# When the modulation rows of a two-layer hybrid are computed: from the first key block on, with a pause before layer 1

## The chip, the cores and the metric

One core of a Trainium2 chip runs the whole program. The metric is the device time of one execution in microseconds; of the kernel before there are three, from 2134.82 to 2137.38 with a median of 2135.68.

## The reference: what is computed

A model of two layers on 256 latent rows and 256 context rows of width 2048, in float32. A vector c modulates both layers: `silu(c)` is multiplied by wide matrices, which gives a shift, a scale and a gate of 2048 numbers for each layer.

```python
h = norm(x) * (1 + scale) + shift          # shift, scale, gate = silu(c) @ ada[layer]
layer 0: q,k,v,z,ab,b,c,h,z2 = h @ w_in    # 16 heads of gated DeltaNet, both directions, and a short convolution
layer 1: chunk MLP (two gelu halves, layer norm over 2048, a 128-row mixing matrix) and a pool of four radii
x = x + gate * (y @ w_out)
```

Layer 1's shift and scale are wanted when layer 1 begins, its gate only in the last output projection.

## The kernel before

Each float32 weight block of 512 KB (a chunk: 128 partitions x 1024) is loaded by a DMA that SyncE issues, split by ScalarE into a high part H (L202) and by VectorE into a low part L = raw - H (L209), and TensorE multiplies three times: H by the high activations, L by the high ones, H by the low ones (L234 in `proj`, L243 to L245 in `projT_n`). `wchunk` does the load and the split for all 554 chunks. In the order of VectorE's list, chunks 0 to 31 are the first projection, 32 to 71 the key and value blocks (`wkv`), 72 to 263 the four head groups of layer 0 (head groups 0 to 3), 264 to 327 its output projection, and the rest is layer 1.

The modulation rows are 256 units in the background of that stream. `ada_step` issues a 256 KB load of 128 rows x 512 columns (L273, SyncE) and, four units behind, one VectorE instruction that multiplies it by silu(c) and adds it to an accumulator (L281; every sixteenth starts one, L279); after 16 units TensorE sums over the partitions (`adc`, L287), ScalarE copies (L289) and a small matmul (L291) and VectorE put the row away. `wchunk` calls it: `tick[0]` is a rate per chunk, taken from `RATE` by stage (`tick[2]`): 0 key blocks, 1 head groups, 2 output projection of layer 0, 3 layer 1. In stage 2 it stops at 198 steps (12*16+2+4), which finish all but layer 1's gate. Before layer 1, L1015 makes up what is missing to 198, since L1016 reads the scale.

The instructions are written in this order, and a scheduler then reorders each engine's list by its own model of times; an engine executes its list in order.

At the layer boundary `out_proj` multiplies the last block by the gate (`opt`, L668), adds it to x (L669) and lets ScalarE square and sum (L670). `row_rstd` (L992, L993, and ten small instructions of `rsqrt`, L337 to L341, 128x1 each) gives the reciprocal root of a row, `dg` (L1022) is a diagonal matrix of it, and TensorE turns x by it (`tr`, L1027); from the turned tile come h, and the first matmuls of layer 1. This is done for the two halves n = 0 and n = 1. At the end of each head group the state scan ends in a chain `z` (L894), `az` (L916), a norm, and the transposes `oT` (L933). In layer 1, `wsT`, `lnw` and `lnb` are loads that GpSimd issues for the layer norm and the mixing (`sp`, L1160).

Of the kernel before, what the change touches and what calls it, by code (L numbers as in the profile page):

```python
# [14 lines left out]
ALU = mybir.AluOpType  # L15
# [4 lines left out]
KT = 16  # L20
# [9 lines left out]
HP = 1  # L30
LA = 4
FINK = 2
RATE = (2.5, 0.6, 1.2, 0.4)
LP = (0.0, 0.0, 0.0, 0.0)
CHUNKS = (1, 2, 4, 4, 5)
RADII = (1, 2, 4, 8)
# [86 lines left out]
def body(ctx: ExitStack, tc: tile.TileContext, T, dbg=None):  # L123
    nc = tc.nc
    dbg = dbg or {}
    V, S, PE, G = nc.vector, nc.scalar, nc.tensor, nc.gpsimd
# [3 lines left out]
    def pool(name, bufs=1, space=None, stack=ctx, side=None):  # L130
        kw = {} if space is None else {"space": space}
        if space is None:
            kw["reuse_waits"] = "tile"
        if side is not None:
            kw["side"] = side
        return stack.enter_context(tc.tile_pool(name=name, bufs=bufs, **kw))
# [56 lines left out]
    tick = [0.0, 0.0, 0, 0.0]  # L193

    def wchunk(src, nk, rp=None, hp=None, lp=None, sz=1024, HL=None):
        if extra[0] and hp is None:
            extra[1] += 1
            rp, hp, lp = extra[0][extra[1] % len(extra[0])]
        raw = (rp or wrawp).tile([P, sz], F32, name="raw", tag="raw")
        dma(raw, src)  # L200
        H = HL[0] if HL else (hp or whp).tile([P, sz], F32R, name="H", tag="H")
        S.copy(H, raw)  # L202
        L = HL[1] if HL else (lp or wlp).tile([P, sz], F32R, name="L", tag="L")
        tick[3] += LP[tick[2]]
        if tick[3] >= 1.0:
            tick[3] -= 1.0
            G.tensor_tensor(L, raw, H, ALU.subtract)
        else:
            V.tensor_tensor(L, raw, H, ALU.subtract)  # L209
        tick[1] += tick[0]  # L210
        while tick[1] >= 1.0:
            tick[1] -= 1.0
            if tick[2] != 2 or ada_n[0] < 12 * KT + FINK + LA:
                ada_step()
        return [t.rearrange("p (k c) -> p k c", k=nk) for t in (H, L)]

# [6 lines left out]
    def proj(src, cols, acts, outs, shared, kts=KT):  # L223
        nk = 1024 // cols
        for c in range(kts // nk):
            H, L = wchunk(src[:, c * 1024:(c + 1) * 1024], nk)
            for kk in range(nk):
                k = c * nk + kk
                for n, o in enumerate(outs):
                    st = k == 0 and n % shared == 0  # L230
                    sp = k == kts - 1
                    wH, wL = (t[:, kk, n * P:(n + 1) * P] for t in (H, L))
                    for i, (w, t) in enumerate(((wH, 0), (wH, 1), (wL, 0))):
                        PE.matmul(o, w, acts(t, k),  # L234
                                  start=st and i == 0, stop=sp and i == 2, skip_group_check=True)
# [31 lines left out]
    araw, aacc, ada_n = {}, {}, [0]  # L267

    def ada_load(u):
        w, col = segs[u // 64][:2]  # L270
        k, col = u % KT, col + u // KT % 4 * 512
        araw[u] = adap.tile([P, 512], F32, name="araw", tag="araw", bufs=LA)
        dma(araw[u], w[k * P:(k + 1) * P, col:col + 512])  # L273

    def ada_acc(u):
        k, raw = u % KT, araw.pop(u)
        if k == 0:
            aacc[u // KT] = adap.tile([P, 512], F32, name="acc", tag="acc", bufs=2)
            V.tensor_scalar(aacc[u // KT], raw, cs[:, 0, 0:1], None, ALU.mult)  # L279
        else:  # L280
            V.scalar_tensor_tensor(aacc[u // KT], raw, cs[:, k, 0:1], aacc[u // KT], ALU.mult, ALU.add)  # L281

    def ada_fin(s):
        out0, gate = segs[s // 4][2:]
        t = gp.tile([P, 132], F32, name="adc", tag="g")
        for n in range(4):
            PE.matmul(t[32 * n:32 * n + 32, 0:P], ones[:, 0:32], aacc[s][:, n * P:(n + 1) * P], start=True, stop=True)  # L287
        ts = adap.tile([P, P], F32, name="ads", tag="ads")
        S.copy(ts, t[:, 0:P])  # L289
        t = t[:, P:132]  # L290
        PE.matmul(t, ts, sel4, start=True, stop=True)  # L291
        c4 = out0 + 4 * (s % 4)
        V.tensor_tensor(modc[:, c4:c4 + 4], t, adabc[:, c4:c4 + 4], ALU.add)
        if gate is not None and s % 4 == 3:
            t = gp.tile([P, P], F32, name="adr", tag="g")
            PE.transpose(t[0:KT], modc[:, out0:out0 + KT], ident)
            r = adap.tile([KT, P], F32, name="arow", tag="ads")
            S.copy(r, t[0:KT])
            dma(rowd[gate].rearrange("(a b) -> a b", a=KT), r)
# [3 lines left out]
    def ada_step(n=1):  # L303
        for _ in range(max(0, min(n, ADA_N - ada_n[0]))):
            u = ada_n[0]
            if u < 256:
                ada_load(u)
            if LA <= u < 256 + LA:
                ada_acc(u - LA)
            f = u - KT - FINK - LA + 1  # L310
            if f >= 0 and f % KT == 0:
                ada_fin(f // KT)
            ada_n[0] += 1
# [54 lines left out]
    with ExitStack() as ph1:  # L368
# [3 lines left out]
        with ExitStack() as ph0:  # L372
# [69 lines left out]
            def k_load(e, j):  # L442
                return [t[:, 0] for t in wchunk(T["wset"][e, j], 1, rp=k0r, hp=whp, lp=wlp, sz=768)]
# [146 lines left out]
        def finish(b, ps):  # L590
            grp, kv, half = b // 4, b // 2 % 2, b % 2
            for n in range(2):
                h = grp * 4 + half * 2 + n
                w = conv5[:, 16 + 16 * kv + h, :]
                ft = cp.tile([P, 512], F32, name="kvT", tag="kvT")
                conv_silu(cp, ft, ps[:, n, :], w, 512)
                tr = gp.tile([P, 4, P], F32, name="kvp", tag="g")
                for m in range(4):
                    PE.transpose(tr[:, m, :], ft[:, m * P:(m + 1) * P], ident)
                tk = cp.tile([P, 4, P], F32, name="kvt", tag="kvt")  # L600
                if kv == 0:
                    dma(ktd[h], ft)
                    S.copy(tk, tr)
                    jk = cp.tile([P, P], F32, name="jk", tag="jk")
                    for m in range(4):
                        S.activation(jk, tk[:, m, :], AF.Square, accum_out=ksq[:, m, h:h + 1])
                    dma(kkd[h], tk.rearrange("p a b -> p (a b)"))
                else:
                    V.tensor_tensor(tk, tr, nrs[:, :, h:h + 1].to_broadcast([P, 4, P]), ALU.mult)
                    dma(vvd[h], tk.rearrange("p a b -> p (a b)"))  # L610
            if b % 4 == 1:
                hs = slice(grp * 4, grp * 4 + 4)
                V.tensor_scalar(kr2[:, :, hs], ksq[:, :, hs], EPS, None, ALU.add)
                rsqrt(nrs[:, :, hs], kr2[:, :, hs])
                V.scalar_tensor_tensor(nrs[:, :, hs], nrs[:, :, hs], -1.0, kr2[:, :, hs], ALU.mult, ALU.mult)
                V.reciprocal(kr2[:, :, hs], kr2[:, :, hs])

        early = [0, 1, 4, 5, 8, 9]
        for step, b in enumerate((12, 13, 2, 3, 6, 7, 10, 11, 14, 15)):
            if step == 3:  # L620
                tick[0], tick[2] = RATE[0], 0
            ps = pj.tile([P, 2, 512], F32, name="pj", tag="pj")
            proj(T["wkv"][b // 4, b // 2 % 2, b % 2], 256, both, [ps[:, n, :].rearrange("p (s t) -> p s t", s=2) for n in range(2)], 1)
            if early:
                finish(early.pop(0), acc[step])
            finish(b, ps)
            if step == 6:
                ab_rows()
                hx = hxp.tile([P, 2, KT, 256], F32R, name="hx", tag="hx")
            if step > 6:  # L630
                for t in range(2):
                    for q in range(1 if step < 9 else 2):
                        k4 = slice(4 * (step - 7 + q), 4 * (step - 6 + q))
                        S.copy(hx[:, t, k4], hxc[:, 0, t, k4])
# [45 lines left out]
    hxH, hxL = hx[:, 0], hx[:, 1]  # L680
    tick[0], tick[2] = RATE[1], 1
    KTp = pool("ktp", 2, stack=y_stack, side="right")
# [304 lines left out]

    tick[0], tick[2] = RATE[2], 2

# [59 lines left out]

    tick[0], tick[2] = RATE[3], 3  # L1050
    Wk = pool("wk1", 2)
# [175 lines left out]
```

## Time and profile before

| | |
|---|---|
| profiled execution: time, span | 2136.03 us, 2134.3 us |
| median of three | 2135.68 us |
| TensorE matmuls busy | 2051.9 us, 96% |
| TensorE weight loads busy | 84% |
| VectorE busy | 1546.9 us, 72% |
| ScalarE busy | 1024.3 us, 48% |
| all loads and stores | 446 MB, mean 209 GB/s |

The time lies 1.7 us above the span. TensorE is idle for 82.4 us of the span. A modulation unit costs VectorE one instruction (`acc`), TensorE next to nothing, and the DMA queue one load. In a timeline a row's time is from its start to its recorded end, and the next may start a little earlier; in the waits the releaser is the instruction whose end let the engine go on.

### The profile page before, as it was taken

To read this page: it belongs to the slowest core of one execution; us is meant where nothing else is said; L and a number is where in the kernel's file an instruction comes from. 1 tells how busy PE (TensorE), PEld (TensorE's weight loads), DVE (VectorE), ACT (ScalarE), POOL (GpSimd) and SP (SyncE) were. 2 spreads that over 40 slices of the span, in tenths; PEclk is the share of its full clock that TensorE was granted. 3 is DMA by queue.
4 is the path that set the end of the run, shared out by engine and by line. 5 is a ranking of instruction groups with operands and counts; after the bars stand their busy time and mean duration, and the time that the engine had idled before them with its cause. 6 is when DMAs were issued, how large, how long until landed. Compare 5 with 4: busy or idle time off the path is not lost. (4 is left out here: it accounts for less than half of the span.)

```text
span 2134.3 us, 37062 instructions
## 1 busy us (share of the span) xinstructions
PE 2051.9 (96%) x14414; PEld 1785.0 (84%) x14414; DVE 1546.9 (72%) x2767; ACT 1024.3 (48%) x1764; POOL 34.0 (2%) x51
## 2 busy tenths in 40 slices
PE   6999999999999999989999999898999999999998
PEld 4667888889999999889999778677888888888886
DVE  4435997877976899579759984798687886665554
ACT  5223366325554556445646554445454555444443
POOL 0000000000000000000000000000010000000000
PEclk9999999999999999999999999999999999999999
DMA  9776745777644785366457752897765666667663
GB/s 347 265 257 211 233 158 187 248 245 268 184 131 147 256 269 159 120 211 186 132 157 245 268 178 70 286 319 270 264 213 168 189 189 198 197 192 222 193 194 131
DMA packets 151248, 446.09 MB, mean 209 GB/s; under 512 B 16512, under 2 KB 23456, under 8 KB 150048
## 3 DMA queue, kind: packets, MB, share of 16 engines
q1 hardware_dynamic: 145936, 425.37, 61.5%
q0 software_dynamic: 5136, 18.35, 2.7%
q8 instruction: 113, 1.85, 0.4%
q14 instruction: 63, 0.52, 0.1%
HBM read 423.19 MB, written 20.46 MB: 208 GB/s over the span
## 5 line engine op out<-in xcount | busy, mean ns | idle before, releaser
L202 ACT CAST H<-raw 128x1024 fp32r<-128x1024 f32 (+1 forms) x554 | 575.3, 1042 | 719.3 <-PE pj L234 215.7
L209 DVE TENSOR_TENSOR L<-raw,H 128x1024 fp32r<-128x1024 f32 (+1 forms) x554 | 667.4, 1207 | 340.6 <-ACT H L202 331.7
L234 PE MATMUL pj<-hx,H 128*128 128x256 f32 x3072 | 562.6, 283 | 0.0
L234 PEld LDWEIGHTS pj<-hx,H 128*128 128x128 f32 x3072 | 476.1, 189 | 3.2 <-issue 0.6
L234 PE MATMUL pj<-hx,L 128*128 128x256 f32 x1536 | 434.9, 283 | 0.0
L1076 PE MATMUL pj<-h,H 128*128 128x512 f32 x1024 | 361.1, 396 | 2.2 <-DVE jn L1085 2.2
L234 PEld LDWEIGHTS pj<-hx,L 128*128 128x128 f32 x1536 | 290.3, 189 | 2.1 <-issue 1.0
L1078 PE MATMUL pj<-h,L 128*128 128x256 f32 x1024 | 287.9, 281 | 0.0
L1076 PEld LDWEIGHTS pj<-h,H 128*128 128x128 f32 x1024 | 192.7, 188 | 46.9 <-DVE jn L1085 2.5
L234 PE MATMUL pj<-hxc,H 128*128 128x512 f32 x640 | 204.9, 399 | 0.0
L281 DVE SCALAR_TENSOR_TENSOR acc<-araw,cs,acc 128x512 f32<-128x512 f32 x240 | 178.8, 745 | 25.3 <-DMA araw<-in_ada 13.7
L1078 PEld LDWEIGHTS pj<-h,L 128*128 128x128 f32 x1024 | 194.2, 190 | 0.2 <-issue 0.2
L234 PEld LDWEIGHTS pj<-hxc,H 128*128 128x128 f32 x640 | 119.5, 188 | 28.2 <-issue 0.8
L234 PE MATMUL pj<-hxc,L 128*128 128x512 f32 x320 | 127.5, 398 | 0.0
L450 PE MATMUL pj<-hxc,H 128*128 128x512 f32 (+1 forms) x272 | 87.6, 397 | 0.0
L243 PE MATMUL pj<-H,y 128*128 128x512 f32 x192 | 76.0, 396 | 0.0
L244 PE MATMUL pj<-L,y 128*128 128x512 f32 x192 | 75.9, 396 | 0.0
L245 PE MATMUL pj<-H,y 128*128 128x512 f32 x192 | 75.9, 396 | 0.0
L234 PEld LDWEIGHTS pj<-hxc,L 128*128 128x128 f32 x320 | 60.3, 188 | 14.0
L450 PEld LDWEIGHTS pj<-hxc,H 128*128 128x128 f32 x272 | 49.8, 193 | 14.4 <-issue 4.5
L387 PE MATMUL adm<-raw,cs 128*32 128x256 f32 x512 | 42.3, 407 | 16.9 <-DMA raw<-in_ada 16.9
L243 PE MATMUL pj<-H,yb 128*128 128x512 f32 x128 | 51.4, 401 | 3.7 <-ACT H L202 2.6
(399 smaller groups left out, 3093.6 us busy)
## 6 DMA issues: line engine op xcount, KB each, us to landing
raw<-in_wbb SPq DMA_DIRECT2D x128, 512.0 KB, 3.8
raw<-in_wout SPq DMA_DIRECT2D x128, 512.0 KB, 3.8
araw<-in_ada SPq DMA_DIRECT2D x192, 256.0 KB, 4.6
raw<-in_ada SPq DMA_DIRECT2D x64, 512.0 KB, 6.5
raw<-in_wpz SPq DMA_DIRECT2D x64, 512.0 KB, 3.7
raw<-in_wuz SPq DMA_DIRECT2D x64, 512.0 KB, 4.2
raw<-in_wkv SPq DMA_DIRECT2D x40, 512.0 KB, 4.4
araw<-in_ada0g SPq DMA_DIRECT2D x64, 256.0 KB, 4.0
```

What stands on the lines that cost most here:

```text
L202: S.copy(H, raw)
L209: V.tensor_tensor(L, raw, H, ALU.subtract)
L234: PE.matmul(o, w, acts(t, k), start=st and i == 0, stop=sp and i == 2, skip_group_check=True)
L243: PE.matmul(o, xH[:, t], H[:, kk, :], start=st, stop=False, skip_group_check=True)
L244: PE.matmul(o, xH[:, t], L[:, kk, :], start=False, stop=False, skip_group_check=True)
L245: PE.matmul(o, xL[:, t], H[:, kk, :], start=False, stop=sp, skip_group_check=True)
L281: V.scalar_tensor_tensor(aacc[u // KT], raw, cs[:, k, 0:1], aacc[u // KT], ALU.mult, ALU.add)
L387: PE.matmul(m[32 * kk:32 * kk + 32, 0:256], cs32[:, 4 * c + kk, :], raw[:, kk * 256:(kk + 1) * 256], start=c == 0, stop=c == 3, skip_group ...
L450: PE.matmul(ps[n].rearrange("p (s t) -> p s t", s=2)[:, q], w_, hxc[:, q, t, j, :], start=first and i == 0 and srcs[0] == 0, stop=last and ...
L1076: PE.matmul(ps[:, n], H[:, kk, w], x[:, :, k, :], start=k == 0, stop=k == kts - 1, skip_group_check=True)
L1078: PE.matmul(ps[:, n, 0], L[:, kk, w], x[:, 0, k, :], start=False, stop=k == kts - 1, skip_group_check=True)
```

## The change

The key blocks start the background steps at the first block (step 0 of the ten) and no longer at the fourth. The limit of 198 steps holds in stages 0, 1 and 2. In stage 3 each step is issued behind the low part of its chunk by `tc.issue_after`, at a rate of one step in two chunks in place of two in five.

```diff
-RATE = (2.5, 0.6, 1.2, 0.4)
+RATE = (2.5, 0.6, 1.2, 0.5)
...
-            V.tensor_tensor(L, raw, H, ALU.subtract)
+            low = V.tensor_tensor(L, raw, H, ALU.subtract)
         tick[1] += tick[0]
         while tick[1] >= 1.0:
             tick[1] -= 1.0
-            if tick[2] != 2 or ada_n[0] < 12 * KT + FINK + LA:
+            if tick[2] == 3:
+                with tc.issue_after(low.ins):
+                    ada_step()
+            elif ada_n[0] < 12 * KT + FINK + LA:
                 ada_step()
...
-            if step == 3:
+            if step == 0:
                 tick[0], tick[2] = RATE[0], 0
```

The scheduler's lists change throughout. Units accumulated when the VectorE list has come to a chunk's low part, before and now: chunk 47: 32 and 32; chunk 60: 45 and 73; chunk 70: 68 and 96; chunk 90: 96 and 127; chunk 262: 165 and 194; chunk 331: 214 and 194; chunk 353: 256 and 205; chunk 455: 256 and 256. Lines of the changed kernel stand three higher behind L216.

VectorE at the layer boundary, before, from the sum of the squares for n = 0 on (`rst` and `rsy` are the small tiles of the reciprocal root, `acc` is a modulation unit, `x_1` the second half):

```order
L992 TENSOR_REDUCE rst_4196<-sq_4195 128x1
L281 SCALAR_TENSOR_TENSOR acc<-araw,cs,acc 128x512
L668 TENSOR_TENSOR opt<-pg,gts 128x512
L209 TENSOR_TENSOR L<-raw,H 128x1024
L993 TENSOR_SCALAR rsq_4197<-rst_4196 128x1
L209 TENSOR_TENSOR L<-raw,H 128x1024
L281 SCALAR_TENSOR_TENSOR acc<-araw,cs,acc 128x512
L669 TENSOR_TENSOR x_1_15075<-x_1_15075,opt 128x512
L337 TENSOR_SCALAR rsy<-rsq_4197 128x1
L281 SCALAR_TENSOR_TENSOR acc<-araw,cs,acc 128x512
L339 TENSOR_TENSOR rst<-rsy 128x1
L992 TENSOR_REDUCE rst_4196<-sq_4195 128x1
```

and now, from the instruction behind that sum to the `dg` of n = 0:

```order
L996 TENSOR_SCALAR rsq_4297<-rst_4296 128x1
L340 TENSOR_SCALAR rsy<-rsq_4297 128x1
L342 TENSOR_TENSOR rst<-rsy 128x1
L343 SCALAR_TENSOR_TENSOR rst<-rst,rsq_4297 128x1
L344 SCALAR_TENSOR_TENSOR rsy<-rst,rsy 128x1
L342 TENSOR_TENSOR rst<-rsy 128x1
L343 SCALAR_TENSOR_TENSOR rst<-rst,rsq_4297 128x1
L344 SCALAR_TENSOR_TENSOR rsy<-rst,rsy 128x1
L342 TENSOR_TENSOR rst<-rsy 128x1
L343 SCALAR_TENSOR_TENSOR rst<-rst,rsq_4297 128x1
L344 SCALAR_TENSOR_TENSOR rst_4296<-rst,rsy 128x1
L1025 TENSOR_SCALAR dg<-cst,rst_4296 128x128
```

Three modulation units, two low parts and the other half's `opt` and `x`, which stand in the first piece, are not between the steps of this chain any more; three low parts and that `opt` and `x` stand behind the `dg`.

TensorE at the end of head group 2, before (`pj` is a projection, `oT` the transposes, `adc` a sum of the modulation rows):

```order
L234 MATMUL pj<-hx,L 128x256
L234 MATMUL pj<-hx,H 128x256 x2
L234 MATMUL pj<-hx,L 128x256
L933 MATMUL oT<-cst,on 128x128 x4
L234 MATMUL pj<-hx,H 128x256
L933 MATMUL oT<-cst,on 128x128 x4
L287 MATMUL adc<-acc,cst 32x128 x8
L234 MATMUL pj<-hx,H 128x256
L234 MATMUL pj<-hx,L 128x256
L234 MATMUL pj<-hx,H 128x256 x2
```

and now (`rq` and `G` are the first matmuls of the next group):

```order
L237 MATMUL pj<-hx,L 128x256
L897 MATMUL z<-r,U 128x128 x4
L919 MATMUL az<-zs,aT 128x128 x4
L936 MATMUL oT<-cst,on 128x128 x8
L290 MATMUL adc<-acc,cst 32x128 x8
L722 MATMUL rq<-qs,cst 32x256 x4
L752 MATMUL G<-KTt 128x128 x4
L294 MATMUL adc<-cst,ads 128x4
L727 MATMUL rq<-cst,rs 128x4 x2
L237 MATMUL pj<-hx,H 128x256 x2
```

The last projection matmul before the next group stands ahead of `z`, `az` and `oT` now, where before projections stood on both sides of `oT`.

## Rows read from the trace of the kernel before

**Rows 1.** The page, part 1: busy time, share, instructions of each engine.

```profile
PE 2051.9 (96%) x14414; PEld 1785.0 (84%) x14414; DVE 1546.9 (72%) x2767; ACT 1024.3 (48%) x1764; POOL 34.0 (2%) x51
```

**Rows 2.** TensorE's waits, whole span: line, releaser; total, times, longest, us.

```profile
PE oT L933 <- DVE on L930: 13.1, 2, 6.6
...
PE Sp L905 <- ACT zk L898: 4.3, 6, 1.6
...
PE az L916 <- ACT zs L901: 2.9, 4, 0.7
...
PE sp L1160 <- DMA wsT<-in_wsT: 2.3, 1, 2.3
```

**Rows 3.** Windows at the layer boundary: busy us (instructions), clock, DMA.

```profile
1437.20:1445.70 8.50, 0.00 (x0) 0.03 (x1) 8.47 (x31) 1.77 (x3) 0.00 (x0) 0.62 0.86 267
1445.70:1449.40 3.70, 3.70 (x17) 3.70 (x18) 1.98 (x5) 0.46 (x1) 0.00 (x0) 0.50 0.80 292
```

**Rows 4.** Groups of VectorE, 360.3 to 372.57: count, busy us, mean ns, idle before.

```profile
L281 DVE SCALAR_TENSOR_TENSOR acc<-araw,cs,acc 128x512 f32<-128x512 f32 x8 | 6.0, 752 | 3.5 <-DMA araw<-in_ada0g 3.3
```

**Rows 5.** Timeline of TensorE across the boundary: start, us, work, idle before.

```profile
1436.76 0.39 PE L245 MATMUL pg<-H,yaL 128*128 128x512 f32 x1
1445.70 5.61 PE L1027 MATMUL tr<-dg,x 128*128 128x128 f32 x32 [8.55 <-issue]
...
1452.49 0.48 PE L243 MATMUL pj<-H,h 128*128 128x512 f32 x1
...
1465.88 0.40 PE L243 MATMUL pj<-H,h 128*128 128x512 f32 x1
```

**Rows 6.** Timeline of ScalarE there, the squares of the last x.

```profile
1435.36 0.62 ACT L670 ACTIVATE opt<-x 128x512 f32<-128x512 f32 x1
```

**Rows 7.** Timeline of VectorE there.

```profile
1434.80 0.74 DVE L281 SCALAR_TENSOR_TENSOR acc<-araw,cs,acc 128x512 f32<-128x512 f32 x1
1435.49 1.22 DVE L209 TENSOR_TENSOR L<-raw,H 128x1024 fp32r<-128x1024 f32 x1
1436.63 0.15 DVE L992 TENSOR_REDUCE rst<-sq 128x1 f32<-128x4 f32 x1
...
1445.31 0.28 DVE L1022 TENSOR_SCALAR dg<-cst,rst 128x128 f32<-128x128 f32 x1
```

**Rows 8.** Timeline of VectorE, a reciprocal root that nothing interrupts.

```profile
1339.13 0.17 DVE L344 TENSOR_SCALAR oss<-oss 128x8 f32<-128x8 f32 x1 [2.59 <-ACT on L925]
...
1341.34 0.17 DVE L928 TENSOR_TENSOR fac<-fac,rqs 128x8 f32<-128x8 f32 x1
```

**Rows 9.** Windows: layer norm, end of head group 1, and twice head group 3.

```profile
1594.00:1611.00 17.00, 11.74 (x51) 9.70 (x50) 10.92 (x22) 4.58 (x6) 3.35 (x7) 0.80 0.57 183
925.00:930.60 5.60, 5.60 (x35) 4.43 (x35) 4.75 (x9) 0.92 (x3) 0.00 (x0) 0.50 0.40 110
1150.00:1170.00 20.00, 20.00 (x164) 19.65 (x163) 20.00 (x50) 12.82 (x40) 0.00 (x0) 1.00 0.78 245
1190.00:1205.00 15.00, 10.93 (x49) 8.29 (x49) 13.85 (x23) 8.53 (x10) 0.00 (x0) 0.89 0.86 290
```

**Rows 10.** Timeline of VectorE, low parts in key blocks and layer 1.

```profile
372.57 1.22 DVE L209 TENSOR_TENSOR L<-raw,H 128x1024 fp32r<-128x1024 f32 x1
...
1557.47 1.23 DVE L209 TENSOR_TENSOR L<-raw,H 128x1024 fp32r<-128x1024 f32 x1 [0.54 <-ACT H L202]
```

**Rows 11.** Timeline of TensorE, where these low parts are first used.

```profile
382.31 0.40 PE L234 MATMUL pj<-hxc,L 128*128 128x512 f32 x1
...
1565.03 0.28 PE L1078 MATMUL pj<-h,L 128*128 128x256 f32 x1
```

**Rows 12.** Timeline of TensorE, end of head group 1.

```profile
924.78 1.94 PE L933 MATMUL oT<-cst,on 128*128 128x128 f32 x8 [6.57 <-DVE on L930]
```

**Rows 13.** Windows: key blocks, then layer 1.

```profile
340.00:360.00 20.00, 20.00 (x93) 16.24 (x93) 13.68 (x25) 11.50 (x31) 0.00 (x0) 1.00 0.46 152
1600.00:1850.00 250.00, 247.33 (x1405) 215.42 (x1404) 182.15 (x278) 122.43 (x159) 3.21 (x6) 0.99 0.60 187
```

## The prediction

> **What bounds the kernel now.** I read the page's busy times first, then what TensorE waits for, then windows and timelines at the waits. The matmuls fill 2051.9 of 2134.3 us [rows 1], so at most 82.4 us of idle can be won, and what a moved instruction is worth is read at the place where TensorE stands still. The list of waits names one engine again and again: the transposes `oT` wait for VectorE twice, 13.1 us in all; the scans' `Sp` and `az` 4.3 and 2.9 us; the mixing matmul `sp` 2.3 us for a load [rows 2]. The largest single wait behind the start is at the layer boundary, put down to "issue", which hides who is late. The window there shows it: between 1437.20 and 1445.70 TensorE did nothing and VectorE was busy for 8.47 of 8.50 us; then the granted clock was 0.50 (1.2 GHz, the lower of its two levels) for 3.7 us, which costs half of that, 1.85 us [rows 3]. So here VectorE sets the end, although TensorE is the busier engine.
>
> **The change part by part.** All sums go against the profiled execution, 2136.03 us (0.35 above the median of 2135.68). Nothing is computed more or less: 256 units before and now. What moves is when VectorE does them, one each about 0.66 us back to back (recorded mean 0.75 [rows 4], and the next starts before a record ends).
>
> *1. The layer boundary.* TensorE's last projection matmul ends at 1437.15, its first `tr` starts at 1445.70 after 8.55 us, the first h matmul comes at 1452.49, and the first chunk that layer 1 loads behind its first three is used at 1465.88 [rows 5]. ScalarE squares x at 1435.36 [rows 6], done with its read of the sum at about 1436.0. VectorE reduces at 1436.63, because an `acc` and a low part stood ahead, and reaches `dg` only at 1445.31 [rows 7]. The list between x and `dg` holds 6 `acc` (4.0 us), 3 low parts (1.14 each, 3.4 us) and `opt` and x of the other half (0.6 each, 1.2 us): 8.6 us that do not belong to the chain. Now none of them stands there. An undisturbed root goes at 0.20 us a step (eleven steps between 1339.13 and 1341.34) [rows 8]; twelve steps from 1436.0 give a `dg` that ends at about 1438.5, so the idle is 1.4 us, 7.1 less. Next late is h: behind the new `dg` stand three low parts, `opt`, x and four halves of `hf` before the first h can be rounded, 3.4 + 1.2 + 4 x 0.33 + small ones and 0.6 for the rounding = 6.9 us, so h comes at 1445.4, and TensorE, done with 16 transposes at 1440.5, waits some 4.9 us. That is 7.1 us earlier than 1452.49. Then 18 matmuls (4.2 us), 16 transposes for the other half (2.0), h of that half (2.5) and 18 matmuls lead to 1458.3 to 1459 for the chunk used at 1465.88, about 7 earlier. Of that about 0.8 us are sums of the modulation rows that only move elsewhere. The clock may fall in the 4.9 us wait as it did after the 8.55: no gain there. I take -6; the ends are -4 (a further low clock of 3.7 us, 1.85) and -10.4 (all 8.55 us and the 1.85 of the clock).
>
> *2. The layer norm of layer 1.* From 1594 to 1611 TensorE was busy 11.74 of 17.00 us at a mean clock of 0.80 [rows 9]: 5.3 us idle and at most 17 x 0.20 = 3.4 of clock, 8.7 in all. 2.3 of it is `sp` waiting for `wsT`, which was scheduled ahead of the layer norm's own loads; now the `sp` stand some fifty chunks later. On the other side eight `acc` (5.3 us) come into the chunks of this stretch, where before all units were done. By the order, with the durations of before, VectorE is asked there for up to 9.3 us more than TensorE takes for the same chunks, against 7.4 before, and the low parts run 6.3 us ahead (1557.47 + 1.23 to 1565.03) [rows 10, 11]: a stall of some 3.4 and a clock cost of 1.8 remain, 5.2 in place of 8.7. I take -3.5, between 0 (the new `acc` eat it) and -8.7.
>
> *3. Ends of head groups.* A group's end with no projection left costs 6.57 us at `oT` [rows 12], 0.73 at `az` (its longest wait) [rows 2], and half of the 5.6 us at clock 0.50 [rows 9], 2.8: 10.1 in all. Before, two ends of four had it. Now the end of group 2 has it too: the last projection matmul stands ahead of `z`. That is +10.1. But the projections held back no longer crowd what follows: in 1150 to 1170 VectorE was busy 20.00 of 20.00 us, and in 1190 to 1205 TensorE stood for 4.07 us with a mean clock of 0.89 (15 x 0.11 = 1.65) [rows 9]. A VectorE that uses the stall to catch up saves most of these 5.7 us; I take -5, net +5, between 0 (those waits vanish and the stall is half hidden by the next group's first matmuls) and +10. In groups 1 and 3 more projections stand between the scans' steps: of the 7.2 us of `Sp` and `az` [rows 2], three uncovered ends keep 0.73 each and one `z`, and I take -4 for the rest, between 0 and -5.
>
> *4. The key blocks.* By chunk 70, 28 units more have been done there, 18.5 us of VectorE; by chunk 90, 31 (20.5). TensorE never waits there, so nothing can be won. What hides it is the lead of the low parts and VectorE's idle time. A burst of eight `acc`, in which VectorE stood 3.3 us behind their loads [rows 4], shows how far the lead falls: the low part behind it started at 372.57 and was done at 373.8 [rows 10], and its first use was at 382.31 [rows 11], 8.5 us later. And VectorE was busy for 13.68 of 20 us in 340 to 360 with TensorE at 20.00 [rows 13]; over about 100 us such idle gives more than 20 us. The ends are 0 and 20.5 - 8.5 + 1.85 = +13.9 (no idle usable). The rows with idle stand nearer: +0.5.
>
> *5. The rest.* Group changes carry some 4 us more of VectorE at leads of 2 us and up: +1 (0 to +3). Layer 1 gets half an `acc` per chunk: 250 us hold 90 chunks, 45 x 0.66 = 30 us on top of 182.15 of 250 [rows 13], still under TensorE's time: 0. The loads move with the units; 0.46 of the DMA engines in 340 to 360 leaves room: 0. The start and the last projection are the same in both: 0.
>
> Sum: -6 - 3.5 + 5 - 4 + 0.5 + 1 = -7.0, so 2129.0 profiled and about 2128.5 as a median.
>
> **A rule against it.** The Trainium skill, Perfetto Trace Analysis, section Identifying the Most-Contended Engine, says to judge VectorE by its busy share and TensorE by that of its weight loads, and to work on the engine with the highest first. That is TensorE here, 84% to 72% [rows 1], and by the rule alone a change that only moves VectorE's instructions leaves 2135.7. The window [rows 3] says otherwise for this stage, and the skill's next section on that page, Optimization Strategy, grants that the contended engine can change over a kernel.
>
> **The rivals.**
> - *A: more is won.* The boundary gives its 10.4 and group 2's stall is covered: 2128.5 - 4.4 - 5 = about 2119. For it: VectorE filled all of the idle. Against it: the low parts that stand right behind `dg`.
> - *B: eaten up.* Group 2's end costs its full 10.1 and the layer norm gives nothing: 2128.5 + 5 + 3.5 = about 2137; with half of these 2133. For it: TensorE waits in 1190 to 1205 for ScalarE too, and these waits need not vanish.
> - *C: slower.* VectorE becomes the bound in the key blocks: its idle there is waiting for buffers that TensorE frees, and then 20.5 us come out of a lead of 8.5: +13.4 over my term, 2141.9. It decides as soon as a low part of chunks 56 to 90 ends behind the matmul that wants it. For it: the lead of 8.5 behind a burst, and the 3.3 us for which the units' own loads held VectorE up. Against it: 6.3 us of VectorE idle in 20, with TensorE full.
> - *D: it does nothing.* The "issue" at the boundary is another delay that VectorE's work only fills, or TensorE's total decides: 2135.7.
>
> **How the numbers follow.** A measurement of this kernel tells about 0.2% (4.3 us) from nothing. Forecast 0.44 (its own range 2124 to 2133), A 0.19, B 0.17, C 0.14, D 0.06. Below 2131.4 lie A, 0.40 of the forecast and 0.03 of B: 0.62. Above 2139.9 lie 0.12 of C and 0.02 of B: 0.14. The rest is 0.24. The range from 2117 to 2139 leaves out a little below A and most of C.
>
> **What would show it.** Right: no `acc` between the last x and `dg`, `tr` within 3 us of the last projection matmul, a second wait of 4 to 6 us for the first h, three waits of 6.6 at `oT` in place of two, no wait of `sp` for `wsT`, a full TensorE between 300 and 450 us. Wrong: `tr` late although VectorE is free (D), TensorE waiting for a low part in the key blocks (C), no third `oT` wait (A), or the waits of group 3 still there (B).

## The result and the profile after

The changed kernel is slower by some 0.6%: 2147.22 us against 2135.68, ratio 1.0061 with a 95% interval of 1.0048 to 1.0074; timed again beside the experiments, 2145.38 against 2132.52, ratio 1.0067 (1.0049 to 1.0085). The forecast was 2128.5. One of its first five executions took 3922 us for a reason that no run shows (2147.22 is the median of five with it, 2146.7 of the other four), and since that was the profiled one, the rows here are from the second timing (span 2148.3 us).

The page of the changed kernel, busy times [rows 1]:

```profile
PE 2057.7 (96%) x14414; PEld 1787.9 (83%) x14414; DVE 1544.8 (72%) x2767; ACT 1023.5 (48%) x1764; POOL 33.9 (2%) x51
```

TensorE's matmuls take 5.8 us more than before and the span is 14.0 us longer: idle grew by 8.2 us, and the 5.8 are put down to the lower clock, since the matmuls are the same 14414 and the mean granted clock fell from 0.986 to 0.980. What TensorE waits for (line, releaser, total, times, longest) [rows 2]:

```profile
PE oT L936 <- DVE on L933: 19.7, 3, 6.6
...
PE pj L1079 <- DVE jn L1088: 10.9, 5, 3.3
...
PE pj L246 <- ACT yb L351: 5.1, 1, 5.1
...
PE rq L722 <- ACT qs L719: 2.0, 1, 2.0
...
PE Sp L908 <- ACT zk L901: 1.0, 2, 0.5
```

A third wait at `oT`, as forecast; `jn` (the join of a pair of results, which frees the buffer that TensorE wrote them to) 10.9 us where the same view of before had 3.0, one wait of 5.1 us for `yb` and one of 2.0 us for `rq`; `Sp` went from 4.3 to 1.0 us. The wait of `tr` at the boundary and that of `sp` for `wsT` are gone. Stage by stage, from the end of one landmark matmul to the next (us; the last rows end at the 7350th and 8600th matmul on a chunk and at the last of all):

| stage | before | changed | difference |
|---|---|---|---|
| to the end of head group 1 | 926.7 | 927.7 | +1.0 |
| head groups 2 and 3 | 417.6 | 431.9 | +14.3 |
| output projection | 92.8 | 91.3 | -1.5 |
| boundary, to the last `tr` | 23.4 | 15.1 | -8.3 |
| value blocks and first pool | 87.6 | 86.8 | -0.8 |
| pool, layer norm, first `sp` | 231.6 | 242.1 | +10.5 |
| to the last matmul on a chunk | 343.9 | 342.8 | -1.1 |

A stage's time also holds work that moved: 36 projection matmuls that stood behind group 2's `oT` before stand ahead of it now. Counted at the same matmul on a chunk, which leaves this out, the changed kernel is 2.4 us late at the 5200th (1027 us before, ahead of group 2's end), 13.1 us at the 6000th (1171 us, behind it) and 14.5 us at the 6700th, in the output projection. So the end of group 2 costs 10.7 us, and the rest of the head groups little.

The boundary gave what was hoped for. TensorE across it [rows 5]:

```profile
1450.45 0.39 PE L248 MATMUL pg<-H,yaL 128*128 128x512 f32 x1
1450.68 3.73 PE L1030 MATMUL tr<-dg,x 128*128 128x128 f32 x32
1456.11 0.50 PE L246 MATMUL pj<-H,h 128*128 128x512 f32 x1 [1.69 <-ACT h L351]
```

`tr` follows the last projection matmul without a pause, and the wait for h is 1.69 us. VectorE there [rows 7]:

```profile
1446.15 0.16 DVE L995 TENSOR_REDUCE rst<-sq 128x1 f32<-128x4 f32 x1 [0.85 <-ACT opt L673]
...
1448.47 0.28 DVE L1025 TENSOR_SCALAR dg<-cst,rst 128x128 f32<-128x128 f32 x1
...
1452.31 1.22 DVE L209 TENSOR_TENSOR L<-raw,H 128x1024 fp32r<-128x1024 f32 x1
...
1456.09 0.69 DVE L352 TENSOR_TENSOR h<-hf,h 128x512 fp32r<-128x512 f32 x1
```

Nothing stands between the sum and `dg`, which is ready 2 us before TensorE asks for it. The three low parts and `opt` behind `dg` are the next late thing, as forecast, but against TensorE's last projection matmul they start earlier than I had them.

The loss starts at the end of group 2. TensorE there and at the first matmul that reads `yb`, in group 3 [rows 12]:

```profile
1145.34 1.94 PE L936 MATMUL oT<-cst,on 128*128 128x128 f32 x8 [6.57 <-DVE on L933]
...
1210.59 0.80 PE L246 MATMUL pj<-H,yb 128*128 128x512 f32 x1 [5.07 <-ACT yb L351]
```

Windows of the key blocks (the first two) [rows 13], behind that `oT` and from the `yb` wait on [rows 9]:

```profile
300.00:450.00 150.00, 150.00 (x723) 119.74 (x721) 135.75 (x291) 74.77 (x160) 0.00 (x0) 1.00 0.78 253
340.00:360.00 20.00, 20.00 (x92) 16.19 (x91) 19.53 (x41) 11.04 (x21) 0.00 (x0) 1.00 0.89 281
1145.40:1149.90 4.50, 4.50 (x36) 3.30 (x37) 3.66 (x6) 0.92 (x3) 0.00 (x0) 0.50 0.20 67
1208.00:1218.20 10.20, 7.08 (x16) 5.11 (x17) 8.22 (x13) 6.65 (x8) 0.00 (x0) 0.50 0.56 174
```

In the key blocks VectorE is now busy 19.53 of 20 us, and TensorE is full over all of 300 to 450: the 28 units make it wait nowhere there. Behind the `oT` the clock is at 0.50, and the wait for `yb` in group 3 comes with 10.2 us at 0.50, where the kernel before had a mean of 0.89 over 15 us at that place, a third of it.

The `yb` that TensorE waits for is a cast on ScalarE, and ScalarE's timeline shows that it stands behind a load:

```profile
1208.55 1.04 ACT L202 CAST H<-raw 128x1024 fp32r<-128x1024 f32 x1 [4.77 <-DMA raw<-in_wout]
1209.50 2.93 ACT L351 CAST yb<-yld 128x1024 fp32r<-128x1024 f32 x3
```

It comes in ScalarE's list behind the H cast of a chunk, which waited 4.77 us for its weights. SyncE issued this load at 1205.07 us, straight behind the end of the low part of an earlier chunk. The last row here is VectorE's:

```profile
1203.82 1.22 DVE L209 TENSOR_TENSOR L<-raw,H 128x1024 fp32r<-128x1024 f32 x1 [1.68 <-ACT H L202]
```

That the load waited for the buffer which this low part frees fits these times, but no run tests it. VectorE itself stood idle for 1.68 us just before.

All of group 3, from group 2's last `oT` to its own, before:

```profile
1131.70:1344.30 212.60, 193.50 (x1584) 168.72 (x1586) 163.70 (x321) 109.41 (x209) 0.75 (x1) 0.97 0.60 193
```

The same stretch in the changed kernel:

```profile
1147.30:1359.60 212.30, 192.71 (x1548) 167.58 (x1552) 150.53 (x300) 107.00 (x205) 0.75 (x1) 0.94 0.52 168
```

VectorE has 13 us less to do there, and yet TensorE idles for 19.6 us where it idled for 19.1, at a mean clock of 0.94 in place of 0.97.

In layer 1, this is one of the long `jn` waits. First VectorE's timeline before 1714 us:

```profile
1711.58 1.23 DVE L209 TENSOR_TENSOR L<-raw,H 128x1024 fp32r<-128x1024 f32 x1 [2.75 <-ACT H L202]
1712.72 0.74 DVE L284 SCALAR_TENSOR_TENSOR acc<-araw,cs,acc 128x512 f32<-128x512 f32 x1
1713.38 0.68 DVE L1088 TENSOR_TENSOR jn<-jn,pj 128x512 f32<-128x512 f32 x1
```

ScalarE's timeline at the same time:

```profile
1710.50 1.05 ACT L202 CAST H<-raw 128x1024 fp32r<-128x1024 f32 x1 [2.39 <-PE pj L1079]
1711.45 0.58 ACT L1084 COPY jn<-pj 128x512 f32<-128x512 f32 x1
```

And TensorE's:

```profile
1714.12 0.50 PE L1079 MATMUL pj<-h,H 128*128 128x512 f32 x1 [2.89 <-DVE jn L1088]
```

TensorE stands 2.89 us for a buffer that the join at 1713.38 frees. That join stands in VectorE's list behind a low part that waited for its H and behind a unit; the H cast at 1710.50 had waited 2.39 us for TensorE to free a buffer, and ScalarE's copy for a join stands behind that cast too. VectorE was idle for 2.75 us just before: it had the time, but its list and ScalarE's had the join behind what waited. The unit itself is only 0.66 us of it.

### The profile page after: what moved, and what is told of

It is laid out like the page before. It is cut to its first block, busy times and chain, and to the rows that moved or that the text cites. A ratio compares the mean times of both kernels' runs of the same rounds, so it can differ in the third digit from the quotient of the medians.

```text
span 3920.3 us, 36990 instructions
## 1 busy us (share of the span) xinstructions
PE 3861.0 (98%) x14414; PEld 2995.6 (76%) x14414; DVE 1562.3 (40%) x2767; ACT 1025.7 (26%) x1764; POOL 34.6 (1%) x51
## 5 line engine op out<-in xcount | busy, mean ns | idle before, releaser
L237 PE MATMUL pj<-hx,H 128*128 128x256 f32 x3072 | 1036.8, 444 | 0.0
L237 PEld LDWEIGHTS pj<-hx,H 128*128 128x128 f32 x3072 | 900.8, 349 | 10.0 <-issue 8.7
L237 PE MATMUL pj<-hx,L 128*128 128x256 f32 x1536 | 680.7, 443 | 0.0
L1079 PE MATMUL pj<-h,H 128*128 128x512 f32 x1024 | 610.9, 613 | 4.7 <-DVE jn L1088 4.7
L237 PEld LDWEIGHTS pj<-hx,L 128*128 128x128 f32 x1536 | 538.5, 351 | 4.0 <-issue 2.6
L1081 PE MATMUL pj<-h,L 128*128 128x256 f32 x1024 | 416.6, 407 | 0.0
L1079 PEld LDWEIGHTS pj<-h,H 128*128 128x128 f32 x1024 | 256.6, 251 | 164.2 <-issue 103.2
L237 PE MATMUL pj<-hxc,H 128*128 128x512 f32 x640 | 368.9, 679 | 0.0
L237 PEld LDWEIGHTS pj<-hxc,H 128*128 128x128 f32 x640 | 188.9, 297 | 101.7 <-issue 94.1
L237 PE MATMUL pj<-hxc,L 128*128 128x512 f32 x320 | 217.1, 678 | 0.0
L453 PEld LDWEIGHTS pj<-hxc,H 128*128 128x128 f32 x272 | 80.6, 310 | 40.5 <-issue 35.4
L453 PE MATMUL pj<-hxc,L 128*128 128x512 f32 (+1 forms) x136 | 88.6, 656 | 0.0
```

Source lines behind the costliest of these rows:

```text
L237: PE.matmul(o, w, acts(t, k), start=st and i == 0, stop=sp and i == 2, skip_group_check=True)
L453: PE.matmul(ps[n].rearrange("p (s t) -> p s t", s=2)[:, q], w_, hxc[:, q, t, j, :], start=first and i == 0 and srcs[0] == 0, stop=last and ...
L1079: PE.matmul(ps[:, n], H[:, kk, w], x[:, :, k, :], start=k == 0, stop=k == kts - 1, skip_group_check=True)
L1081: PE.matmul(ps[:, n, 0], L[:, kk, w], x[:, 0, k, :], start=False, stop=k == kts - 1, skip_group_check=True)
```

## Experiments

Each was timed in five rounds beside the kernel before, whose median differs from set to set (2132.5 to 2134.8 us); so runs of different sets are compared by what each lies over or under the kernel before. "End of group 3" is the end of its last `oT` in the profile: 1344.3 us before, 1359.6 in the changed kernel.

**e1_after.** No edit.

> The changed kernel itself, for a profile at full pace. Both theories: 2143 to 2149 us, as timed. Theory 1 (the loss is in the key blocks and head groups): a third wait of 6.6 us at oT, further waits of TensorE for low parts or for VectorE in 300 to 1350, together 15 us or more over before, and the boundary shorter by 5 to 8 us. Theory 2 (the loss is in layer 1): the time up to the last out_proj matmul is within 3 us of before (1437), and the stretch from there to the end is 10 us or more longer.

Measured 2145.38 us; its profile is the one above. Both are there: group 3 ends 15.3 us later, and layer 1 gives back what the boundary gained (8.6 us against 8.3). Theory 1 is right on the place of the larger part, theory 2 on a second one.

**e2_early_start.** The kernel before with the early start alone.

```diff
-            if step == 3:
+            if step == 0:
```

> The kernel before with only the start of the background steps moved from the fourth key block to the first. Theory 1: slower than the changed kernel, some 2150 to 2156 us, since the loss is here and the gain of the boundary is not. Theory 2: no change, 2133 to 2138 us.

2152.2 us, ratio 1.0093 (1.0072 to 1.0114); group 3 ends at 1357.6. Its waits at `oT`, `tr` and `sp`:

```profile
PE oT L933 <- DVE on L930: 19.7, 3, 6.6
...
PE tr L1027 <- issue: 13.1, 1, 13.1
...
PE sp L1160 <- DMA wsT<-in_wsT: 6.5, 1, 6.5
```

Theory 1 holds for this part: the early start by itself costs 13.3 us up to the end of group 3, and it made the boundary's wait longer (13.1 in place of 8.5), since nine units and three low parts stand between the last x and `dg` in its list, in place of six and three.

**e3_layer1_only.** The changed kernel with the late start.

```diff
-            if step == 0:
+            if step == 3:
```

> The changed kernel with the start put back to the fourth key block: the limit of 198 steps in every stage, the steps of layer 1 behind the low parts, rate 0.5. VectorE's and TensorE's lists up to the end of the head groups are those of before. Theory 1: faster than before by 6 to 9 us, 2127 to 2130 us. Theory 2: as slow as the changed kernel, 2143 to 2149 us.

2133.93 us, ratio 1.0006 (0.9992 to 1.0020). Neither theory's time came: boundary 15.1 us in place of 23.4, but the pool stretch 240.1 in place of 231.6. Its waits at `oT` and for `jn`:

```profile
PE oT L936 <- DVE on L933: 13.1, 2, 6.6
PE pj L1079 <- DVE jn L1088: 10.6, 5, 3.3
```

So the gain of the boundary is taken back within layer 1. By the medians, each against the kernel before, the early start alone costs 19.7 us, layer 1's part alone 1.4, and both together 12.9: the limit spares the early start the long boundary wait of e2.

**e4_cover.** Group 2 gets a block of group 3.

```diff
-FCUT = (0, 3, 7, 12, 16)
+FCUT = (0, 3, 7, 13, 16)
```

> The changed kernel with one block of projections more in head group 2 (FCUT 0, 3, 7, 13, 16 in place of 0, 3, 7, 12, 16): up to group 1's end all lists are those of the changed kernel, and at group 2's end projections stand on both sides of oT again. Theory G (the loss of the head groups is the end of group 2 left without projections): two oT waits of 6.6 us in place of three, and 8 to 14 us faster than the changed kernel, 2131 to 2138 us. Theory V (VectorE lags because of the units put into the key blocks): no such gain, 2142 to 2148 us.

2145.03 us, 1.0062 (1.0044 to 1.0080). The third `oT` wait is gone and little is won: in the profile group 3 ends at 1355.3, and by the medians the whole is 11.6 us over the kernel before, where the changed kernel is 12.9. Its waits at `oT` and in the inverses:

```profile
PE oT L936 <- DVE on L933: 13.1, 2, 6.6
...
PE X L833 <- issue: 8.0, 4, 4.1
...
PE X L859 <- ACT PTq L853: 2.4, 1, 2.4
```

Three of the `X` waits, 5.9 us together, lie in group 3's inverses between 1293 and 1305 us, where the changed kernel waits 2.2 us: they miss the block that went to group 2. Theory G in this plain form falls; theory V is not shown by it either.

**e5_slow_start.** The changed kernel with a slower pace in the key blocks.

```diff
-RATE = (2.5, 0.6, 1.2, 0.5)
+RATE = (1.5, 0.6, 1.2, 0.5)
```

> The changed kernel with the background steps from the first key block on, but at 1.5 a chunk in place of 2.5: the units done by the end of the key blocks are about those of the kernel before (66 by chunk 70, where before had 68), while group 2's end is left without projections as in the changed kernel. Theory G: as slow as the changed kernel, 2142 to 2148 us, with the third oT wait. Theory V: as the variant with layer 1's part alone, 2131 to 2137 us.

2147.38 us, 1.0076 (1.0053 to 1.0099), group 3 ends at 1355.3. Its `oT` waits:

```profile
PE oT L936 <- DVE on L933: 19.7, 3, 6.6
```

With the units of the key blocks back at about the number of before, group 3 still ends 11 us late and the time is no better (13.9 us over the kernel before): theory V falls.

**e6_l1_fast.** e3 with a faster pace in layer 1.

```diff
-RATE = (2.5, 0.6, 1.2, 0.5)
+RATE = (2.5, 0.6, 1.2, 1.5)
```

> Layer 1's part alone (start at the fourth key block) with 1.5 steps a chunk in layer 1 in place of 0.5, so that the gate's units are done by chunk 400 and not by 455. Theory L (the units beside the pool's and the layer norm's work hold up the joins that free PSUM): the waits for jn go down from 10.6 to some 6 us and the time is 3 to 6 us below the variant at 0.5, 2127 to 2131 us. Rival (the waits come from the place where the joins stand in the list, whatever the units): 2133 to 2136 us.

2120.33 us, ratio 0.9948 (0.9930 to 0.9965), 13.1 us under the kernel before: more than theory L said. Its waits:

```profile
PE oT L936 <- DVE on L933: 13.1, 2, 6.6
...
PE pj L1079 <- DVE jn L1088: 1.3, 1, 1.3
```

The window from 1690 to 1760 us in e3:

```profile
1690.00:1760.00 70.00, 63.38 (x358) 54.83 (x358) 56.30 (x92) 29.58 (x40) 2.16 (x4) 0.95 0.65 209
```

The same window in e6, where the units are done by 1570 us:

```profile
1690.00:1760.00 70.00, 69.70 (x399) 60.78 (x398) 55.68 (x85) 35.93 (x45) 1.07 (x2) 1.00 0.62 194
```

And in the kernel before, where they are done by 1519 us:

```profile
1690.00:1760.00 70.00, 69.71 (x401) 61.00 (x400) 55.99 (x88) 35.50 (x46) 0.00 (x0) 1.00 0.61 188
```

VectorE has as much to do in all three windows (56.3, 55.7 and 56.0 of 70 us), but with units it has other lists, and TensorE's idle time is 6.3 us longer. The pool stretch is 226.5 us in place of 240.1, nearly all of the 14.5 us between e6 and e3.

**e7_gate_late.** e3 with no unit before the `wuz` blocks.

```diff
-    tick[0], tick[2] = RATE[3], 3
+    tick[0], tick[2] = 0.0, 3
...
+    tick[0] = 1.1
     for gi in range(16):
```

> Layer 1's part alone, with no step in layer 1 before the wuz blocks and then 1.1 a chunk: none of the gate's units stands in the value, pool and layer norm stretches. Theory L: no more than 5.7 us of idle between the pool's start and the middle of wuz, the boundary's 8 us kept, 2123 to 2128 us. Rival: the joins still wait 10 us, 2132 to 2136 us.

2126.84 us, 0.9970 (0.9957 to 0.9983). The pool stretch is 227.3; the last stretch is 347.1, some 3 us longer than before, where the units went. Its `jn` waits, all but 0.81 us of them before 1593 us:

```profile
PE pj L1079 <- DVE jn L1088: 5.2, 3, 2.7
```

**e8_rate055.** e6 with another pace in the head groups.

```diff
-RATE = (2.5, 0.6, 1.2, 1.5)
+RATE = (2.5, 0.55, 1.2, 1.5)
```

> Layer 1's part at 1.5 a chunk (the run before of 2120 us), with 0.55 in place of 0.6 steps a chunk in the head groups and nothing else: the units of the key blocks are the same (96 by chunk 90 and by 140), but the new list of TensorE ends group 2 in z, az, oT without projections between. Theory S (the head groups of the kernel before owe their time to one list that any small change loses; the early start only loses it): head groups 2 and 3 together take 427 to 432 us in place of 417 to 419, and the whole 2129 to 2134 us. Theory V (units in the key blocks): no change, 2118 to 2123 us.

2128.3 us, 0.9975 (0.9963 to 0.9987), 6.5 us under the kernel before where e6 is 13.1 under; groups 2 and 3 take 427.5 us in place of 419.3, though group 1 ends 3.8 us earlier. Its `oT` waits:

```profile
PE oT L936 <- DVE on L933: 20.7, 3, 7.6
```

Theory S is borne out in the stage, with a whole just under its range: up to the key blocks' end all units are those of e6, and a small change of pace loses the cover of group 2's end and with it 6.6 us by the medians (the profiled spans, one execution each, differ by 4.3).

**e10_both_fast.** The changed kernel with e6's pace.

```diff
-RATE = (2.5, 0.6, 1.2, 0.5)
+RATE = (2.5, 0.6, 1.2, 1.5)
```

> The changed kernel with 1.5 in place of 0.5 steps a chunk in layer 1. If the costs of the two parts add up, it is 13 us faster than the changed kernel, 2130 to 2134 us, about the kernel before. Rival (layer 1's gain hangs on the list of the kernel before): 2138 to 2146 us.

2134.61 us, 0.9999 (0.9988 to 1.0010). Against the kernel before that is 13.0 us better than the changed kernel, where e6 is 14.5 better than e3: the parts nearly add up, and the early start with a good pace in layer 1 is no better than the kernel before.

**e11_phase.** e3 with the units behind the other chunk of each two.

```diff
-    tick[0], tick[2] = RATE[3], 3
+    tick[0], tick[1], tick[2] = RATE[3], tick[1] + 0.5, 3
```

> Layer 1's part at 0.5 a chunk, with the phase shifted by one chunk: the units stand behind the even chunks and no longer directly ahead of the joins of chunks 399, 417 and 435. Theory P (a unit directly ahead of a join makes TensorE wait for the PSUM that the join frees): waits for jn go down from 10.6 to 5 us or less, 2123 to 2129 us. Theory L (units anywhere in the pool's stretch): 2132 to 2136 us.

2134.58 us, 1.0000 (0.9989 to 1.0011); the same pool stretch (238.8) with the same idle of 10.6 us. Its waits for `jn`, 8.4 us in place of 10.6, with 2.2 us behind a split of y besides:

```profile
PE pj L1079 <- DVE jn L1088: 8.4, 6, 2.2
```

Theory P falls as the cause of the whole. Two of the waits show what the unit is worth. In e3, TensorE's timeline has:

```profile
1691.63 0.50 PE L1079 MATMUL pj<-y,H 128*128 128x512 f32 x1 [0.84 <-DVE jn L1088]
...
1698.26 0.50 PE L1079 MATMUL pj<-h,H 128*128 128x512 f32 x1 [2.89 <-DVE jn L1088]
```

And in e11, for the same two joins:

```profile
1692.87 0.51 PE L1079 MATMUL pj<-y,H 128*128 128x512 f32 x1 [1.50 <-DVE jn L1088]
...
1698.84 0.50 PE L1079 MATMUL pj<-h,H 128*128 128x512 f32 x1 [2.23 <-DVE jn L1088]
```

In VectorE's list the unit stands straight ahead of the second join in e3 and of the first in e11. It takes its own 0.66 us with it from one wait to the other; the 2.2 us that are left of the second stay, whichever join the unit is put ahead of.

**e12_l1_r10.** e3 at 1.0 steps a chunk.

```diff
-RATE = (2.5, 0.6, 1.2, 0.5)
+RATE = (2.5, 0.6, 1.2, 1.0)
```

> Layer 1's part at 1.0 a chunk, a unit behind every low part until about chunk 395. Theory L: between the runs at 0.5 and 1.5, 2121 to 2130 us, with 1 to 6 us of waits for jn. Theory P: units directly ahead of every join until chunk 395, so 2126 to 2136 us.

2129.77 us, 0.9979 (0.9966 to 0.9991). Its waits in the pool stretch:

```profile
PE pj L1079 <- DVE jn L1088: 3.8, 1, 3.8
PE pj L1079 <- DVE modc L296: 3.2, 1, 3.2
```

The time lies in the range of both theories. Both waits come before 1632 us, about where the units end, and none behind; between 1640 and 1760 e3 has four and e11 five, and e6 and e7, whose units are done or begin only at 1739 us, none over 0.81. So in these runs the loss goes with units beside the later rounds of the pool. It also goes with another order: at 0.5 steps a chunk (the changed kernel, e3, e4, e5, e11) the first `sp` starts at 1733 us or later, in all other runs at 1576 to 1652. No run has the one without the other, so it isn't shown which of the two the waits need.

**e13_cover_g0, e14_cover_g1.** e10 with group 2's extra block from group 0 or group 1.

```diff
-FCUT = (0, 3, 7, 12, 16)
+FCUT = (0, 2, 6, 12, 16)    # e13
+FCUT = (0, 3, 6, 12, 16)    # e14
```

> The changed kernel at 1.5 steps a chunk in layer 1, with the projection blocks dealt 2, 4, 6, 4 to the head groups in place of 3, 4, 5, 4 (FCUT 0, 2, 6, 12, 16): group 2's end has projections on both sides of oT again, group 3 keeps its four blocks, and the block comes from group 0, whose end still has projections ahead of oT. Theory G2 (the early start costs the cover of group 2's end, and a block from where it is not needed gives it back): the end of group 3 comes 8 to 14 us earlier than with 3, 4, 5, 4, the whole 2121 to 2127 us. Theory K (the scans and inverses want more projections than there are, so that a block moved only moves the wait): 2131 to 2138 us.

> The same with the block taken from group 1 (3, 3, 6, 4; FCUT 0, 3, 6, 12, 16), whose end is without projections in every kernel so far. Theory G2: as the other, 2121 to 2127 us, or a few us more, for group 1's last steps. Theory K: 2131 to 2138 us, with group 1 longer in its waits by what group 2 saves.

e13: 2128.0 us, 0.9979 (0.9968 to 0.9990), group 3 ends at 1354.1. e14: 2125.87 us, 0.9971 (0.9959 to 0.9982), group 3 ends at 1345.7.

The `oT` waits of e13:

```profile
PE oT L936 <- DVE on L933: 19.5, 3, 6.6
```

And of e14:

```profile
PE oT L936 <- DVE on L933: 13.1, 2, 6.6
```

From group 1 the block gives 7.0 us back, each against the kernel before (0.2 us under it in e10, 7.2 in e14): its end is without projections anyway. From group 0 a third `oT` wait comes up there, and group 3 ends only 3 us earlier than in e10; the whole is 5.0 us under the kernel before, and its interval overlaps that of e14. Theory G2 holds for e14, theory K has its part in e4 and e13.

**e15_l1_r20.** e3 at 2.0 steps a chunk.

```diff
-RATE = (2.5, 0.6, 1.2, 0.5)
+RATE = (2.5, 0.6, 1.2, 2.0)
```

> Layer 1's part alone at 2.0 steps a chunk (start at the fourth key block): the units are done a few chunks before those at 1.5. Theory L: within 3 us of the run at 1.5, 2117 to 2123 us. If the loads of 512 KB a chunk more are too much for the DMA queues, raw blocks come late and it is slower, 2125 to 2135 us.

2119.98 us, 0.9947 (0.9932 to 0.9962), level with e6 (both 13.1 us under the kernel before): the loads are not too much. These two are the fastest of all runs.

At 1.5 steps a chunk in layer 1 the head groups make a table of four, in us under the kernel before that was timed beside each:

| | group 2's end with projections | without |
|---|---|---|
| late start | e6 13.1 | e8 6.5 |
| early start | e14 7.2 | e10 0.2 |

Losing the cover costs 6.6 and 7.0 us; the early start costs a further 5.9 and 6.3. The four intervals are 2 to 4 us to either side.

## Why the prediction was wrong

The sum was -7.0; it came out at +14.0 in the profiles. Two failed steps weigh most: the time that was to be won back behind the end of group 2, and the half unit per chunk that was to cost layer 1 nothing. Term by term:

- **Boundary, -6: right in kind, -8.3 in the table.** What the trace corrects is the second wait, 4.9 us forecast and 1.69 measured. The squares were ready 4.7 us before TensorE was done, and not 1 us, and the sixteen transposes (32 matmuls in the rows) take 3.73 us at the full clock, where the sum had 2.0.
- **Group 2's end, +10.1 for the wait: right; the -5 behind it: wrong.** By the count of matmuls on chunks the end of the group costs 10.7 us. This is the first step that failed: "A VectorE that uses the stall to catch up saves most of these 5.7 us". VectorE did have 13 us less to do in group 3, but TensorE idled as long as before: it kept a wait of 5.07 us for `yb`, behind a weight load, with three times as long at 0.50. Rival B had this, and priced the whole too low.
- **Groups 1 and 3, -4: the waits went, the time did not.** `Sp` waits 1.0 in place of 4.3 us, but most of that was group 3's (3.3 us), which idles as long as before, and group 1's end comes 1.0 us later than before, with a new wait of 2.03 us at `rq` near 511 us. e4 and e13 show the pattern: there are too few projections for all chains, and covering one uncovers another.
- **Key blocks, +0.5: right.** TensorE was busy for all of 300 to 450 us, with VectorE at 19.53 of 20 us in 340 to 360, and rival C did not come. Its number, 2141.9, is the nearest of all to the result, by chance. e5 shows that the number of units there is not the cause of the loss.
- **Layer norm, -3.5, and the rest of layer 1, 0: wrong, +10.5 together.** The step that failed is "45 x 0.66 = 30 us on top of 182.15 of 250 [rows 13], still under TensorE's time: 0". The share of busy time left out the order of the list: VectorE was idle ahead of the join that TensorE wanted, and `jn` cost 10.9 us in place of 3.0. The `sp` wait did go, as forecast. e6 against e3 shows that the pace alone decides over 14.5 us. (The stall in this term, 9.3 less 6.3, is 3.0 and not 3.4, which changes little.)

What stays open: the 6 us that the early start costs beside the cover. e5 speaks against the number of units in the key blocks by chunk 70, but no run tells which of the many moved instructions it is. That the kernel before has its group 2 covered is a fortunate list: every run with another start or pace of the background steps up to the head groups, and the blocks dealt as before (the changed kernel, e2, e5, e8, e10), ends group 2 without projections.

## What to carry to other kernels

Where a scheduler orders the work, read what a change does to the lists far from the edit, and look in them for the instruction that frees a buffer behind one that waits: an engine with idle time can still be late. In these runs, background work that had to be deferred went best where it was done quickly (e6, e15) and not spread thin over everything (e3). Independent work that covers serial chains is a budget: before moving a piece, look for the chain that is uncovered anyway, and take it from there.

## What the hardware did that I had not expected

The lower clock is not a fixed price per wait. A wait of 3.34 us for the same join, at the same place of TensorE's list, which is the same in both from layer 1 on, was followed by the full clock (1.00) in e3 and by the half clock (0.50) in the changed kernel. The window around it in e3:

```profile
1584.00:1594.00 10.00, 6.66 (x37) 5.44 (x36) 9.80 (x15) 4.22 (x6) 1.39 (x3) 1.00 0.94 315
```

The windows up to its end and behind it in the changed kernel:

```profile
1598.40:1601.90 3.50, 0.16 (x2) 0.10 (x1) 3.50 (x6) 1.73 (x3) 0.05 (x1) 0.80 0.80 256
1601.90:1607.20 5.30, 5.30 (x17) 4.53 (x18) 5.30 (x9) 0.60 (x2) 0.69 (x2) 0.50 0.95 361
```

At a later wait of 2.89 us it is the other way round: behind it the L1079 matmuls take 0.63 us each in e3 and 0.40 in the changed kernel. The Trainium skill, TensorE: Matmul & The Clock Gate, Part 1, says that idleness gates the clock down and activity brings it back. The rows agree in kind, and also show that two waits of one length need not have the same cost; after the 5.07 us wait the half clock lasted to the end of a 10.2 us stretch. No run here shows what decides between the cases.
